# Two places for the transposed probabilities around the values' result, and another order of loads and of tiles 14 and 15, in a transformer layer

## The chip, the core and the metric

The kernel runs on one core of a Trainium2 chip. The metric is the device time of one execution in microseconds (us). Its engines are TensorE (PE; PEld is its weight load), VectorE (DVE), ScalarE (ACT), GpSimd (POOL) and SyncE (SP), whose queue issues the loads and stores (DMAs). Each engine takes its instructions in program order.

## What is computed

One layer over 2048 frames of 1024 channels, in float32. The input is scaled and shifted by vectors made from a conditioning vector c, and one projection makes u (512 channels) and q, k, v (8 heads of 64).

```python
h = x * (1.0 + sc1) + sh1
proj = h @ w_in                       # u, q, k, v
y_pool = pool_mixer(u, w_pool, pool_scale)                        # trailing means of 2/4/8/16 frames minus u
y_attn = chunked_attention(q, k, v, rel_bias)                     # 64-frame chunk: itself and 8 chunks before
y = concat([y_pool, y_attn]) @ w_out
x = layer_norm(ALPHA * x + (1.0 + g1) * y, ln1_g, ln1_b)
h = x * (1.0 + sc2) + sh2
f = jnp.square(relu(h @ w_ff1)) @ w_ff2
x = layer_norm(ALPHA * x + (1.0 + g2) * f, ln2_g, ln2_b)
```

## The kernel before

**Numbers.** Every float32 product is made of three matmuls: an operand is kept as a high part (a ScalarE copy to the matmul's rounded type) and a low part (source minus high part, on VectorE or GpSimd). `split` does both.

**Stages.** (1) `load0`, `chain0`, `fold0`, `dense0`: the modulation vectors and the first three blocks of the projection, `FIRST` = A0 (q and k of head 0), V0 (v of heads 0 and 1), U0, over the first 1024 frames. (2) Attention, together with the rest of the projection: a main loop over 128 units (two halves `hf` of 1024 frames, 8 heads, 8 query tiles of 128 frames). (3) `w_out`, residual and first layer norm for 16 tiles of 128 frames (`residual`, `ln1_head`, `ln1_turn`, `ln1_sums`). (4) The MLP in two phases of products over quarters (Strassen-like sums: 7 products for 8), 32 groups of the first one, `product(g, s)` with s from 0 to 6.

**The attention loop.** All order is written by hand: one iteration issues, for unit n, the scores of unit n + 3 (`scores`: S in PSUM, VectorE's reduction L611 into s and m, ScalarE's exponential L613), `normalise` on GpSimd, some matmuls of the projection taken from the generator `dense()` by `step`, then `transposes(n)` (up to five 128x128 blocks of s into T), in even iterations `values(n - 2)` (the product with v for the pair of units before, into pv, 256 columns), then `probs(n)` (high part of T on ScalarE, L635, low part on VectorE, L636, into PT), in even iterations `combine(n - 2)` (ScalarE copies rows 64 to 128 of pv to `yl`, L659; VectorE adds rows 0 to 64, L660), and more of `step`. `evac` brings a projection block out of its bank d in steps: for an A block ScalarE copies q (L300) and k (L301), VectorE makes the low parts (L303, L306).

**PSUM.** Eight banks of 512 float32 columns: left pool psL has d (three of one bank) and T (two banks, one buffer), right pool psR has S (two banks, one buffer) and pv (one bank). The MLP opens `psF0` in psR's place and, some products later, `psF1` in psL's place; `fbank()` deals their eight banks out in turn.

**Pieces.** While the projection's last blocks of the first half run, `h_pieces(tb)` replaces the modulated input in SBUF by that of the second half: a load into `xr` (four buffers), scale and shift (L271), high part (L273), low part (L275), 16 pieces in all, advanced at every second k of a projection block. `wo_pieces(n)` does the same for the scaled output weight `woS`, 8 pieces for each half n. `extras` makes further modulation vectors and `woS` in pieces that use `xr` as well.

**Tiles 14 and 15.** The layer norm of the last tiles overlaps the MLP's first group: `ln1_turn(t)` transposes tile t into T and writes the modulated h with eight ScalarE instructions (L832), `ln1_sums(t)` makes four VectorE sums and stores them, `op_split(i)` splits the operand of product i.

Of the kernel before, what the change touches and what calls it, by code (L numbers as in the profile page):

```python
# [8 lines left out]
F32 = mybir.dt.float32  # L9
# [15 lines left out]
def trunk_layer(ctx: ExitStack, tc: tile.TileContext, xT, x, wada1, wada2, vecs, rows, win, wfirst, wpT, wout,  # L25
# [111 lines left out]

    def dbank():
        return pp.tile([128, 512], F32, name="d", tag="d", bufs=3)

    def wide(tag):
        return (pr if tag == "S" else pp).tile([128, 1024], F32, name=tag, tag=tag, bufs=1)

    def narrow(w=512):
        return pr.tile([128, w], F32, name="pv", tag="pv", bufs=1)
# [7 lines left out]
             (2, 1): narrow()}  # L153
# [11 lines left out]
    def dense0(k):  # L165
        for i, (a, b) in enumerate(((0, 0), (1, 0), (0, 1))):
            for c in range(NF0):
                for tb in range(2):
                    nc.tensor.matmul(first[c, tb], wf[:, a, k, c, :], hT(b, k, slice(tb * 512, tb * 512 + 512)),  # L169
                                     start=(k == 0 and i == 0), stop=(k == 7 and i == 2))  # L170
# [81 lines left out]
    def xr_tile():  # L252
        while stores:
            stores.pop(0)()
        return ap.tile([128, 512], F32, name="xr", tag="xr", bufs=4)

    def h_pieces(tb):
        c0, cols = 1024 + tb * 512, slice(tb * 512, tb * 512 + 512)
        rs = {}

        def load(k):
            rs[k] = xr_tile()
            nc.sync.dma_start(rs[k], xT[k, :, c0:c0 + 512])

        for k in range(4):
            load(k)
        yield
        for k in range(10):
            if k < 8:
                r = rs[k]  # L270
                nc.gpsimd.tensor_scalar(r, r, mod1[:, k, 1:2], mod1[:, k, 0:1], op0=ALU.mult, op1=ALU.add)  # L271
            if 1 <= k < 9:
                nc.scalar.copy(hT(0, k - 1, cols), rs[k - 1])  # L273
            if k >= 2:
                nc.vector.tensor_sub(hT(1, k - 2, cols), rs.pop(k - 2), hT(0, k - 2, cols).bitcast(F32))  # L275
                if k + 2 < 8:
                    load(k + 2)
            if k < 7 or k == 9:
                yield
# [86 lines left out]
    for c, name in enumerate(FIRST):  # L366
        alloc(0, name[0], int(name[1]))
        g = both(c, name)
        pend.append((g, (0, name), name[0]))
# [30 lines left out]
    def dense():  # L400
        w, open_, side = {}, [], iter(())
        for hf, name, tb in blocks():
# [10 lines left out]
            prep = st.split_some(open_[0] + 2)  # L413
            if (hf, name, tb) in ((0, "U1", 1), (1, "A0", 0), (1, "A0", 1), (1, "U0", 1)):
                run(side)
                side = iter(()) if (hf, name, tb) == (1, "A0", 1) else wo_pieces(0) if (hf, name) == (1, "U0") else h_pieces(hf)
                next(side, None)
# [203 lines left out]
    def transposes(n):  # L621
        hf, h, i = units[n]
        s, m, nk = P.pop(n)
        e = i % 2
        t = wide("T")
        for j in range(nk):
            nc.tensor.transpose(t[:, j * 128:j * 128 + 128], s[:, j * 128:j * 128 + 128], ident)  # L627
        return t, e, nk
# [9 lines left out]
    def values(n):  # L638
        hf, h, i = units[n]
        gi = hf * 8 + i  # L640
        lo = 4 - min(gi, 4)
        pv = narrow(256)
        v = Vt[hf, h // 2]
        tot = 2 * (6 - lo)
        c = 0
        for sl in range(lo, 6):
            for a in range(2):
                nc.tensor.matmul(pv, v[:, i + sl, h % 2, :], PTt[:, a, sl, :], start=(c == 0), stop=(c == tot - 1))  # L648
                c += 1
        return pv  # L650
# [16 lines left out]
    def wo_pieces(n):  # L667
        run(ex[0])
        run(ex[1])
        flush()  # L670
        cols = slice(n * 512, n * 512 + 512)
        rs = {}

        def load(k):
            rs[k] = xr_tile()
            nc.sync.dma_start(rs[k], woS[k, :, cols])

        for k in range(4):
            load(k)
        yield  # L680
        for k in range(8):
            r = rs.pop(k)
            split(hT(0, k, cols), hT(1, k, cols), r, nc.vector if k % 2 else nc.gpsimd)
            if k + 4 < 8:
                load(k + 4)
            yield
# [137 lines left out]
    def ln1_turn(t, bank="T"):  # L824
# [6 lines left out]
        for k in range(8):  # L831
            nc.scalar.activation(h[:, k, :], pt[:, k * 128:k * 128 + 128], AF.Identity, bias=b2[:, k:k + 1],  # L832
                                 scale=a2[:, k:k + 1])
# [84 lines left out]
    q3 = [s3[:, 0:512], s3[:, 512:1024], narrow()]  # L918
# [89 lines left out]
    op_load(6)  # L1008
    op_split(4)
    ln1_sums(14, 1)  # L1010
# [12 lines left out]
    def fbank():  # L1023
        i = turn[0] % 8
        turn[0] += 1
        return pf[i >= 3].tile([128, 512], F32, name="f", tag="f", bufs=(3, 5)[i >= 3])
# [163 lines left out]
    for g in range(32):  # L1190
        for s in range(7):
            product(g, s)
            tick()
            if g == 0:
                if s == 1:
                    ln1_load(15)
                elif s == 2:
                    ln1_turn(15)
                elif s == 3:
                    ln1_sums(15, 1)  # L1200
                elif s == 4:
                    op_split(6)
                elif s == 5:
                    flush()
# [25 lines left out]
            evacuate(g, s)  # L1230
            if (g, s) == (0, 0):
# [214 lines left out]
```

## Time and profile before

| | |
|---|---|
| median of 3 runs | 2112.88 us (2112.39 to 2114.71) |
| the profiled execution | 2112.46 us, of which the span of instructions is 2110.6 |
| TensorE busy | 2037.9 us (97%) |
| VectorE, ScalarE, GpSimd busy | 1303.0, 1001.5, 333.3 us |

A busy TensorE is not one at its peak, since matmuls are pipelined and their ends are modelled. Idle time of an engine counts when the engine that sets the end waits for it. Start times in rows count from the start of the span.

### The profile page before, as it was taken

What the parts mean: (1) busy time and instruction counts of PE and PEld (TensorE: products, weight loads), DVE (VectorE), ACT (ScalarE), POOL (GpSimd) and SP (SyncE); (2) the same over time, 40 slices, a digit from 0 to 9 for tenths busy, and PEclk for the clock granted to TensorE, in tenths of its full rate; (3) what the DMA queues carried; (4) which work ended last, traced back from release to release, by engine and by line L of the source; (5) the groups of instructions that cost most, each with busy time, mean ns of one, the idle gap of its engine ahead of it and who ended that gap; (6) DMA issues with size and microseconds to landing.
All of it is one profiled execution on the core that took longest, in us unless ns stands there. A gap on an engine that the chain in (4) does not pass through costs nothing.

```text
span 2110.6 us, 27080 instructions
## 1 busy us (share of the span) xinstructions
PE 2037.9 (97%) x9672; PEld 1681.5 (80%) x9672; DVE 1303.0 (62%) x1958; ACT 1001.5 (47%) x1592; POOL 333.3 (16%) x442
## 2 busy tenths in 40 slices
PE   7999989999998999899999999999999999999998
PEld 6778868887877888678888788888788888888886
DVE  7555555556665464767776765666694447775448
ACT  5554555554553555545555655545453333333330
POOL 1535463553333100000000000000000001000002
PEclk9999999999999999999999999999999999999999
DMA  7444444434434678879878988887886556776552
GB/s 300 142 133 127 148 138 112 140 103 141 129 109 125 199 232 296 287 253 324 287 270 296 319 280 295 294 293 281 322 288 211 189 194 209 246 242 227 193 170 110
DMA packets 210360, 456.68 MB, mean 216 GB/s; under 512 B 18609, under 2 KB 36529, under 8 KB 209202
## 3 DMA queue, kind: packets, MB, share of 16 engines
q1 hardware_dynamic: 210226, 454.96, 64.2%
q8 instruction: 76, 1.25, 0.2%
q14 instruction: 58, 0.48, 0.1%
HBM read 294.45 MB, written 152.05 MB: 212 GB/s over the span
## 4 chain that ended last, share of the span: by engine, by line
PE 81%; DVE 7%; ACT 4%; DMA 3%; issue 3%; POOL 2%; SPq 0%; DVEq 0%; POOLq 0%; ACTq 0%
PE f L1331 26%; PE f L1049 26%; PE d L422 10%; PE d L386 6%; PE pv L648 3%; PE T L627 2%; PE S L604 2%; DVE s L611 1%; ACT PT L635 1%; PE d L169 1%; DMA raw<-in_wada_dram 1%; DVE PT L636 1%; DVE sb L60 1%; PE S L169 1%; PE S L386 1%
## 5 line engine op out<-in xcount | busy, mean ns | idle before, releaser
L1331 PE MATMUL f<-sb,sa 128*128 128x512 f32 x2688 | 616.3, 391 | 2.1 <-DVE sb L60 1.8
L1331 PEld LDWEIGHTS f<-sb,sa 128*128 128x128 f32 x2688 | 504.7, 188 | 113.6 <-DVE sb L60 2.5
L422 PE MATMUL d<-hT,hl 128*128 128x512 f32 x1392 | 373.5, 400 | 1.9 <-ACT vt L317 1.9
L1049 PE MATMUL f<-h,hl 128*128 128x512 f32 x1536 | 363.0, 391 | 2.0 <-ACT c L1056 1.2
L1049 PEld LDWEIGHTS f<-h,hl 128*128 128x128 f32 x1536 | 287.9, 188 | 67.9 <-ACT c L1056 2.1
L1049 PE MATMUL f<-sb,hl 128*128 128x512 f32 x1152 | 279.7, 396 | 11.6 <-ACT c L1056 8.1
L422 PEld LDWEIGHTS d<-hT,hl 128*128 128x128 f32 x1392 | 249.2, 190 | 42.2 <-ACT vt L317 2.3
L1049 PEld LDWEIGHTS f<-sb,hl 128*128 128x128 f32 x1152 | 218.0, 190 | 63.0 <-ACT c L1056 9.4
L636 DVE TENSOR_TENSOR PT<-T,PT 128x640 fp32r<-128x640 f32 (+4 forms) x128 | 94.9, 741 | 217.2 <-ACT PT L635 215.1
L613 ACT ACTIVATE s<-s,m 128x640 f32<-128x640 f32 (+4 forms) x128 | 97.9, 765 | 221.3 <-DVE m L611 171.2
L386 PE MATMUL d<-hT,hl 128*128 128x512 f32 x696 | 165.7, 394 | 0.0
L1071 ACT ACTIVATE g<-g 128x512 f32<-128x512 f32 x96 | 60.8, 633 | 210.5 <-DVE g L1062 210.5
L59 ACT CAST sb<-hl 128x1024 fp32r<-128x1024 f32 x67 | 70.4, 1051 | 177.7 <-PE f L1331 142.9
L386 PEld LDWEIGHTS d<-hT,hl 128*128 128x128 f32 x696 | 129.0, 188 | 26.9
L60 DVE TENSOR_TENSOR hl<-wsum,hl 128x1024 fp32r<-128x1024 f32 x64 | 78.4, 1225 | 92.9 <-ACT hl L59 92.9
L619 POOL TENSOR_SCALAR s<-s,m 128x640 f32<-128x640 f32 (+4 forms) x128 | 97.1, 759 | 240.0 <-DVE m L618 192.5
L60 DVE TENSOR_TENSOR sb<-hl,sb 128x1024 fp32r<-128x1024 f32 x67 | 81.9, 1222 | 69.0 <-ACT sb L59 68.8
L59 ACT CAST sb<-raw 128x1024 fp32r<-128x1024 f32 x53 | 55.5, 1052 | 119.2 <-PE f L1331 85.0
L1374 POOL TENSOR_SCALAR ag<-ag 128x1024 f32<-128x1024 f32 x1 | 1.1, 1060 | 666.9 <-DMA ab<-in_rows_dram 666.9
L604 PE MATMUL S<-k,q 128*128 128x320 f32 (+1 forms) x448 | 92.2, 322 | 12.8 <-DVE m L611 12.7
L1300 POOL TENSOR_SCALAR zv<-zv 128x1 f32<-128x1 f32 x16 | 16.7, 1042 | 554.7 <-DVE zv L1299 554.7
L60 DVE TENSOR_TENSOR hl<-w,hl 128x1024 fp32r<-128x1024 f32 x64 | 61.3, 958 | 68.3 <-ACT hl L59 68.3
(182 smaller groups left out, 2674.7 us busy)
## 6 DMA issues: line engine op xcount, KB each, us to landing
fS<-g SPq DMA_DIRECT2D x224, 256.0 KB, 3.9
hl<-fS SPq DMA_DIRECT2D x67, 512.0 KB, 4.7
hl<-tS SPq DMA_DIRECT2D x67, 512.0 KB, 4.7
w<-in_w_dram SPq DMA_DIRECT2D x48, 512.0 KB, 4.3
raw<-fS SPq DMA_DIRECT2D x45, 512.0 KB, 4.6
raw<-tS SPq DMA_DIRECT2D x45, 512.0 KB, 4.8
wS<-wsum SPq DMA_DIRECT2D x32, 512.0 KB, 4.8
raw<-in_w_dram SPq DMA_DIRECT2D x32, 512.0 KB, 5.2
```

The source lines that it names most:

```text
L59: nc.scalar.copy(hl_h, src)
L60: low.tensor_sub(hl_l, src, hl_h.bitcast(F32))
L386: nc.tensor.matmul(ps, yc[:, a, k, :], hT(b, k, cols), start=(k == 0 and i == 0), stop=(k == 7 and i == 2))
L422: nc.tensor.matmul(ps, w[name][:, a, k, :], hT(b, k, slice(tb * 512, tb * 512 + 512)), start=(n == 0), stop=(n == 23))
L604: nc.tensor.matmul(S[:, 512 * p:512 * p + wp], q[:, i * 128:i * 128 + 128], k[:, a, k0 + p * wp:k0 + p * wp + wp], start=(a == 0), stop=(a ...
L613: nc.scalar.activation(s[:, 0:w], s[:, 0:w], AF.Exp, bias=m[:, 0:1], scale=-1.0, accum_out=m[:, 1:2])
L619: nc.gpsimd.tensor_scalar(s[:, 0:nk * 128], s[:, 0:nk * 128], m[:, 1:2], 1.0, op0=ALU.mult, op1=ALU.mult)
L636: nc.vector.tensor_sub(ol, src, oh.bitcast(F32))
L648: nc.tensor.matmul(pv, v[:, i + sl, h % 2, :], PTt[:, a, sl, :], start=(c == 0), stop=(c == tot - 1))
L1049: nc.tensor.matmul(ps, w[:, p, c:c + 128], h[:, q, k, :], start=first and k == 0 and (p, q) == (0, 0), stop=k == 3 and p == 1, skip_group_ ...
L1071: nc.scalar.activation(o, o, AF.Relu)
L1331: nc.tensor.matmul(bank, f, w, start=start, stop=stop, skip_group_check=True)
```

## The change

In PSUM, left and right change places in part. The left pool holds one tile of three banks in a row, `tpv` (1536 columns). In attention the transposes of an even unit go to columns 0 to 640, those of an odd one to 896 to 1536, and the values' result to 640 to 896 between them; elsewhere columns 0 to 1024 serve as T and 1024 to 1536 as the single bank. The d banks move to the right pool; `fbank()` takes five banks from the right pool first and three from the left later.

V0's products end first in the last step of `dense0`, and its evacuation is first in line. `xr` has eight buffers. The pieces of x are loaded eight ahead, the first eight at the block before, and modulated on VectorE, not on GpSimd; those of the output weight are loaded eight ahead over both halves. A piece that is done loads the one six further on, into the buffer freed two pieces before. The sums of tile 14 stand before `op_split(4)`. The turn of tile 15 moves by one product, its eight ScalarE instructions follow that product's evacuation, and its sums and the closing of the pools move after `op_split(6)`.

```diff
+    tpv = pp.tile([128, 1536], F32, name="tpv")
     def dbank():
-        return pp.tile([128, 512], F32, name="d", tag="d", bufs=3)
+        return pr.tile([128, 512], F32, name="d", tag="d", bufs=3)
     def wide(tag):
-        return (pr if tag == "S" else pp).tile([128, 1024], F32, name=tag, tag=tag, bufs=1)
-    def narrow(w=512):
-        return pr.tile([128, w], F32, name="pv", tag="pv", bufs=1)
+        return pr.tile([128, 1024], F32, name="S", tag="S", bufs=1) if tag == "S" else tpv[:, 0:1024]
...
     def dense0(k):
+        order = [(i, c, tb) for i in range(3) for c in range(NF0) for tb in range(2)]
+        if k == 7:
+            order = [(i, c, tb) for c in (1, 0, 2) for tb in range(2) for i in range(3)]
...
-        return ap.tile([128, 512], F32, name="xr", tag="xr", bufs=4)
+        return ap.tile([128, 512], F32, name="xr", tag="xr", bufs=8)
+    def pieces(source):
+        rs = {}
+        def load(j):
+            if j < 16:
+                rs[j] = xr_tile()
+                nc.sync.dma_start(rs[j], source(j))
+        def pop(j):
+            rs.pop(j)
+            if j >= 2:
+                load(j + 6)
+        return rs, load, pop
+    hp_rs, hp_load, hp_pop = pieces(lambda j: xT[j % 8, :, 1024 + j // 8 * 512:1536 + j // 8 * 512])
+    wp_rs, wp_load, wp_pop = pieces(lambda j: woS[j % 8, :, j // 8 * 512:j // 8 * 512 + 512])
     def h_pieces(tb):
-        for k in range(4):
-            load(k)
         yield
         for k in range(10):
             if k < 8:
-                nc.gpsimd.tensor_scalar(r, r, mod1[:, k, 1:2], mod1[:, k, 0:1], op0=ALU.mult, op1=ALU.add)
+                nc.vector.tensor_scalar(r, r, mod1[:, k, 1:2], mod1[:, k, 0:1], op0=ALU.mult, op1=ALU.add)
...
-    for c, name in enumerate(FIRST):
+    for c, name in sorted(enumerate(FIRST), key=lambda v: (1, 0, 2)[v[0]]):
...
+            if (hf, name, tb) == (0, "A7", 0):
+                for j in range(8):
+                    hp_load(j)
...
-        t = wide("T")
+        t = tpv[:, 896 * e:896 * e + 640]
...
-        pv = narrow(256)
+        pv = tpv[:, 640:896]
...
     def wo_pieces(n):
+        if n == 0:
             run(ex[0]); run(ex[1]); flush()
+            for j in range(8):
+                wp_load(j)
...
+    ln1_sums(14, 1)
     op_split(4)
-    ln1_sums(14, 1)
...
-        return pf[i >= 3].tile([128, 512], F32, name="f", tag="f", bufs=(3, 5)[i >= 3])
+        return pf[i >= 5].tile([128, 512], F32, name="f", tag="f", bufs=(5, 3)[i >= 5])
...
             if g == 0:
-                elif s == 2:
-                    ln1_turn(15)
                 elif s == 3:
-                    ln1_sums(15, 1)
+                    turned = ln1_turn(15, later=True)
                 elif s == 4:
                     op_split(6)
                 elif s == 5:
+                    ln1_sums(15, 1)
+                elif s == 6:
                     flush()
                     psL.__exit__(None, None, None)
...
             evacuate(g, s)
+            if (g, s) == (0, 3):
+                turned()
```

## Rows read from the trace of the kernel before

**Rows 1.** The page, its head

```profile
span 2110.6 us, 27080 instructions
```

**Rows 2.** TensorE's waits, whole span: us in total, times, longest us

```profile
PE T L627 <- DVE PT L636: 13.5, 16, 2.5
PE S L604 <- DVE m L611: 12.7, 12, 2.2
...
PE f L1049 <- ACT c L1056: 9.3, 3, 5.8
...
PE d L422 <- ACT vt L317: 1.9, 1, 1.9
```

**Rows 3.** Windows: us, busy PE, PEld, DVE, ACT, POOL, clock, DMA share, GB/s

```profile
282.00:331.00 49.00, 39.02 (x195) 32.14 (x194) 27.40 (x60) 27.48 (x57) 30.41 (x36) 0.93 0.59 164
619.00:663.00 44.00, 38.77 (x226) 32.88 (x225) 25.97 (x50) 24.84 (x48) 24.20 (x27) 0.99 0.41 126
```

**Rows 4.** TensorE's waits from 284 to 345

```profile
PE S L604 <- DVE m L611: 3.5, 2, 2.2
PE T L627 <- DVE PT L636: 3.5, 2, 2.5
PE T L627 <- POOL hl L60: 3.3, 2, 3.0
```

**Rows 5.** Line 271 (min/median/max ns); what it waited for, who waited for it

```profile
L271 POOL TENSOR_SCALAR xr<-xr,mod x16: 763/774/1435, 282.9 to 329.2; 128x512 f32<-128x512 f32 x16
...
  DMA xr<-in_xT_dram: 9.2, 4
...
  ACT hT L273: 13.9, 10
```

**Rows 6.** Line 488, the same operation and shape on VectorE

```profile
L488 DVE TENSOR_SCALAR xa<-xr,cs x6: 469/478/506, 83.3 to 544.9; 128x512 f32<-128x512 f32 x6
```

**Rows 7.** Line 303: what VectorE sat idle for before it

```profile
  ACT k L301: 21.6, 30
```

**Rows 8.** Order of time at 402: start, us, engine, line, operation

```profile
401.92 0.37 ACT L659 COPY yl<-pv 64x256 f32<-64x256 f32 x1
401.93 0.82 DVE L636 TENSOR_TENSOR PT<-T,PT 128x640 fp32r<-128x640 f32 x1 [1.70 <-ACT PT L635]
402.67 0.41 DVE L660 TENSOR_TENSOR y<-pv,yl 64x256 f32<-64x256 f32 x1
...
403.09 0.71 PE L627 MATMUL T<-ident,s 128*128 128x128 f32 x5
```

**Rows 9.** Order of time at 392, two units earlier

```profile
392.04 0.82 DVE L636 TENSOR_TENSOR PT<-T,PT 128x640 fp32r<-128x640 f32 x1 [2.52 <-ACT PT L635]
...
394.53 0.71 PE L627 MATMUL T<-ident,s 128*128 128x128 f32 x5
```

**Rows 10.** TensorE's waits from 635 to 672

```profile
PE T L627 <- DVE PT L636: 5.2, 4, 2.3
```

**Rows 11.** Tile xr, 600 to 670: one wait of ScalarE for it

```profile
  DMA xr<-woS: 4.8, 3
```

**Rows 12.** Order of time at the MLP's entrance

```profile
843.39 5.88 PE L1049 MATMUL f<-h,hl 128*128 128x512 f32 x25
...
845.42 1.28 DVE L873 SCALAR_TENSOR_TENSOR xt<-xt,d 128x512 f32<-128x512 f32 x2
...
854.62 0.68 DVE L1062 TENSOR_TENSOR g<-f,c 128x512 f32<-128x512 f32 x1
...
857.14 2.90 ACT L832 ACTIVATE h<-T,b,a 128x128 f32<-128x128 f32 x8 [3.69 <-DMA hP<-h]
...
859.89 0.66 ACT L1071 ACTIVATE g<-g 128x512 f32<-128x512 f32 x1
...
862.26 4.47 PE L1049 MATMUL f<-sb,hl 128*128 128x512 f32 x12 [5.84 <-ACT c L1056]
...
870.47 3.00 PE L1049 MATMUL f<-sb,hl 128*128 128x512 f32 x12 [0.98 <-DVE g L1062]
```

More of the change, by code (lines that the diff above doesn't have):

```diff
@@ L152, in trunk_layer @@
     first = {(0, 0): s0[:, 0:512], (0, 1): s0[:, 512:1024], (1, 0): dbank(), (1, 1): dbank(), (2, 0): dbank(),
-             (2, 1): narrow()}
+             (2, 1): tpv[:, 1024:1536]}
     ld = {}
@@ L165, in dense0 @@
     def dense0(k):
[L166 to L170, printed above, removed]
+        order = [(i, c, tb) for i in range(3) for c in range(NF0) for tb in range(2)]
+        if k == 7:
+            order = [(i, c, tb) for c in (1, 0, 2) for tb in range(2) for i in range(3)]
+        for i, c, tb in order:
+            a, b = ((0, 0), (1, 0), (0, 1))[i]
+            nc.tensor.matmul(first[c, tb], wf[:, a, k, c, :], hT(b, k, slice(tb * 512, tb * 512 + 512)),
+                             start=(k == 0 and i == 0), stop=(k == 7 and i == 2))
     acs = {}
@@ L254, in xr_tile @@
             stores.pop(0)()
-        return ap.tile([128, 512], F32, name="xr", tag="xr", bufs=4)
-    def h_pieces(tb):
[L258 to L263, printed above, removed]
-        for k in range(4):
-            load(k)
+        return ap.tile([128, 512], F32, name="xr", tag="xr", bufs=8)
[12 more added lines that the diff above has]
+    wp_rs, wp_load, wp_pop = pieces(lambda j: woS[j % 8, :, j // 8 * 512:j // 8 * 512 + 512])
+    def h_pieces(tb):
+        cols = slice(tb * 512, tb * 512 + 512)
         yield
@@ L269, in h_pieces @@
             if k < 8:
-                r = rs[k]
-                nc.gpsimd.tensor_scalar(r, r, mod1[:, k, 1:2], mod1[:, k, 0:1], op0=ALU.mult, op1=ALU.add)
+                r = hp_rs[8 * tb + k]
+                nc.vector.tensor_scalar(r, r, mod1[:, k, 1:2], mod1[:, k, 0:1], op0=ALU.mult, op1=ALU.add)
             if 1 <= k < 9:
-                nc.scalar.copy(hT(0, k - 1, cols), rs[k - 1])
+                nc.scalar.copy(hT(0, k - 1, cols), hp_rs[8 * tb + k - 1])
             if k >= 2:
-                nc.vector.tensor_sub(hT(1, k - 2, cols), rs.pop(k - 2), hT(0, k - 2, cols).bitcast(F32))
-                if k + 2 < 8:
-                    load(k + 2)
+                j = 8 * tb + k - 2
+                r = hp_rs[j]
+                nc.vector.tensor_sub(hT(1, k - 2, cols), r, hT(0, k - 2, cols).bitcast(F32))
+                hp_pop(j)
             if k < 7 or k == 9:
@@ L667, in wo_pieces @@
     def wo_pieces(n):
-        run(ex[0])
-        run(ex[1])
-        flush()
         cols = slice(n * 512, n * 512 + 512)
[L672 to L679, printed above, removed]
+        if n == 0:
+            run(ex[0])
+            run(ex[1])
+            flush()
+            for j in range(8):
+                wp_load(j)
         yield
         for k in range(8):
[L682 to L685, printed above, removed]
+            split(hT(0, k, cols), hT(1, k, cols), wp_rs[8 * n + k], nc.vector if k % 2 else nc.gpsimd)
+            wp_pop(8 * n + k)
             yield
@@ L822, in ln1_load, with ln1_turn @@
             nc.sync.dma_start(hps[t], hP[b][0][r - 4])
-    def ln1_turn(t, bank="T"):
+    def ln1_turn(t, bank="T", later=False):
         n = n_tiles.pop(t)
@@ L830, in ln1_turn, with affine @@
         hts[t] = h = h_tile(t, "h")
-        for k in range(8):
-            nc.scalar.activation(h[:, k, :], pt[:, k * 128:k * 128 + 128], AF.Identity, bias=b2[:, k:k + 1],
-                                 scale=a2[:, k:k + 1])
+        def affine():
+            for k in range(8):
+                nc.scalar.activation(h[:, k, :], pt[:, k * 128:k * 128 + 128], AF.Identity, bias=b2[:, k:k + 1],
+                                     scale=a2[:, k:k + 1])
+        if later:
+            return affine
+        affine()
     def ln1_sums(t, delay=12):
@@ L917, in trunk_layer @@
     s3 = wide("S")
-    q3 = [s3[:, 0:512], s3[:, 512:1024], narrow()]
+    q3 = [s3[:, 0:512], s3[:, 512:1024], tpv[:, 1024:1536]]
     for t in range(3):
```

## The prediction, made before the changed kernel was run

> **What bounds the kernel now.** I read the page's head first, then TensorE's waits over the whole span, then the same waits cut to the stretches in which the diff puts an edit, and last the order of time around single waits. The span is 2110.6 us [rows 1]; the profiled execution took 2112.46 us, 0.42 under the median of 2112.88, and every sum below is made against 2112.46. TensorE is the engine that sets the end, so a microsecond saved elsewhere counts only where TensorE stands still for it. The waits in reach are: 13.5 us of the probabilities' transposes (T) for VectorE's low part of the unit before (PT, L636), 12.7 us of the scores for VectorE's reduction, 9.3 us of MLP products for a ScalarE copy, 1.9 us of a projection for the copy `vt` [rows 2]. The MLP phases, from 843.39 on [rows 12] six tenths of the span, are touched at their entrance alone. A measurement of this kernel tells about 0.2% (4.2 us) from no change.
>
> **Start.** The kernel's first projection to need a bank waits 1.9 us for `vt` [rows 2], which ScalarE makes third, behind A0's two copies. V0 now comes first: two of three about equal copies leave the front, 2/3 x 1.9 = 1.3 saved. At most 1.9, at least 0 (the other copies may then be waited for). The reordered k = 7 products are the same 18 matmuls: nothing.
>
> **The x pieces (282 to 331).** TensorE's waits from 284 to 345 sum to 3.5 + 3.5 + 3.3 = 10.3 us [rows 4], and the granted clock's mean over 282 to 331 is 0.93 [rows 3], where 7% of 49 us is another 3.4 us of work at full speed. What stands behind them: the modulation (L271) runs on GpSimd, 16 times at 774 ns or more, waits 9.2 us for loads, and ScalarE waits 13.9 us for it [rows 5]; ScalarE's queue also holds the next PT copy, VectorE waits for that, and T for VectorE. The change removes the 16 GpSimd instructions, loads eight pieces one block ahead, and reloads two slots behind the one just freed, so that SyncE's queue need not stand on a buffer just being released. It adds 16 VectorE tensor_scalars of the same 128x512 shape, 478 ns by L488 [rows 6]: 7.6 us. Nothing hides these fully: VectorE goes from 27.4 to 35.0 us busy in that stretch, and TensorE needs 39.0 - 3.4 = 35.6 [rows 3]. On SyncE's queue eight loads move ahead of one block's copies and stores; their buffers are free, so they hold it for eight issues only, and the copies of k, wanted a block later, are covered by that block's matmuls (uncovered, they would add a wait for scores). The least it can shrink to is 35.6 of 49, which agrees with 10.3 + 3.4 = 13.7 as the most that is saved. Two engines of equal load that wait for each other in queues don't close up entirely; the other end is VectorE's own 7.6 in TensorE's path, with only the 3.3 that [rows 4] put down to GpSimd itself bought back: +4 (a loss). I take 5 saved: ScalarE's wait of 13.9 goes, VectorE's 7.6 comes, and the difference, 6.3, is shortened for the reductions (L611) that now queue behind a modulation on VectorE and that the scores wait for.
>
> **The output weight's pieces (619 to 663).** Four T waits, 5.2 us together, lie from 635 to 672 [rows 10]; ScalarE waits 4.8 us in 3 cases for the scaled weight's load [rows 11], with the PT copy behind it in its queue. Work on the engines stays as it was; loads go out eight deep and the second half's during the first. VectorE has room (25.97 of 44 [rows 3]). Gain between 0 and 5.2; I take 3.5, since the fourth wait comes after the loads are in.
>
> **Tiles 14 and 15 at the MLP's entrance.** Today the fifth product of the first group waits 5.84 us and starts at 862.26. The copy of c that it waits for stands on ScalarE behind eight affine instructions (2.90 us from 857.14), which themselves waited for the store of tile 14, and behind the square pair that starts at 859.89 [rows 12]. After the change the affine stands behind the copy of the fourth product. The square then follows VectorE's sum of 854.62 + 0.68 = 855.30; from square to product it takes 862.26 - 859.89 = 2.37 today, so the fifth product starts at 857.67. What is late next is the seventh: today 862.26 + 8.21 = 870.47 [rows 12]. The four VectorE sums of tile 15 (0.68 each, like the sum at 854.62), 2.7 in all, leave its path for a place behind the evacuation; the affine and one copy (2.90 + 0.6) enter ScalarE's queue ahead of the split that the seventh needs. 857.67 + 8.21 - 2.7 + 3.5 = 866.7: 3.8 saved. The sums of tile 14 before op_split(4) send the stores of tile 14 some 2.5 us earlier, which covers the slot that the affine writes. The other bound is in the banks: the first five MLP banks now take the place of S and of the three d banks, which the residual of tile 15 reads until 845.42 + 1.28 = 846.70, while the first product starts at 843.39 [rows 12]. If the first product gets one of these, 3.3 of the 3.8 are lost again. S was allocated before d, so I take it that it doesn't.
>
> **The two fields.** T(even) takes columns 0 to 640, the values' result 640 to 896, T(odd) 896 to 1536: the middle bank of 512 holds the last transpose of even units, the values' result, and the first transpose of odd ones. What the trace shows of neighbours in a bank: VectorE's q (L303) reads rows 0 to 64 of d and needs ScalarE's first copy alone, yet 30 times it waits for the second copy (L301), which reads the other rows: 21.6 us [rows 7]. So I take accesses of two engines to one bank to be kept in program order, reads included. Then an even unit that waits for PT(n-1) gets its first four transposes out early, 4/5 of 0.71 = 0.57 at most, while the fifth and the values wait as before. An odd unit gets worse: `yl` may read only when L636 is done (today both start at 401.92) and L660 follows; T(odd), which today needs L636 alone, needs both. That is 0.37 + 0.41 = 0.78 later [rows 8]. Where TensorE leads it costs nothing: 392.04 + 0.82 to 394.53 are 1.67 to spare [rows 9]. Where the spare is 0.34 (402.75 to 403.09 [rows 8]) it costs 0.44. Behind the waiting `yl` stand the next evacuation copies and the exponential on ScalarE. Of 16 waits [rows 2] 2 + 4 are counted in the two stretches above; 10 x 0.57 = 5.7 relief, against some ten tight pairs at 0.44 to 0.78, about 6.5. Net +1; bounds -7 (no cost, also 16 x 0.44 of relief) and +12.5 (16 x 0.78, no relief).
>
> The Trainium skill has the rule in its page "PSUM — Partial Sum Buffer", section "PSUM bank collisions raise a hardware error": two engines may not touch the same bank in the same 32 partitions at once, reads against reads and other columns included, so waits are to be set by bank. This speaks against a layout with a shared middle bank. By this rule the term is the +1 above, and by columns alone it would be about -6; the trace's row agrees with it, and is even stricter, as its two readers use different partitions.
>
> **Sum.** -1.3 - 5 - 3.5 - 3.8 + 1 = -12.6; 2112.46 - 12.6 = 2099.9, said as 2100. The extra attention slots (xr 8 for 4) in the weight extras are costed at nothing: their loads are issued two jobs ahead and lie under projections; if that cover is gone the cost is at most a stall as now.
>
> **The rivals.**
> - Both stretches close up to TensorE's pace: 13.7 and 5.2 in place of 5 and 3.5: 2112.46 - 1.3 - 13.7 - 5.2 - 3.8 + 1 = 2089.5. For it: the waits shown have GpSimd and loads behind them, and both go. Against it: VectorE at 35.0 beside TensorE's 35.6.
> - The fields part by columns: term -6 for +1, 2093. Against it: [rows 7].
> - VectorE becomes the bound of the x stretch (+4 there): 2112.46 - 1.3 + 4 - 3.5 - 3.8 + 1 = 2108.9, within 0.2%. For it: 7.6 us more in its queue, in front of L611.
> - The change doesn't do what it says, that is, the loads and GpSimd were hidden by the same VectorE chain, and both stretches stay: 2112.46 - 1.3 - 3.8 + 1 = 2108.4, at the edge of no change. Against it: the 9.2 and 4.8 us of waits for loads.
> - Slower: the combination enters the loop of every pair. At 0.78 for 40 of 64 pairs (128 units) it costs 31, in place of 1: 2130. It decides from 18 over the gains' 13.6 + 4.2, which is 23 tight pairs. For it: the order in [rows 7]. Against it: only 16 T waits in 128 units, and 1.67 of room in the steady ones.
>
> **Chances.** Forecast 0.46, closing up 0.2, columns 0.1, VectorE bound 0.1, stretches stay 0.08, slower 0.06. The forecast's own range is 2092 to 2107. The two cases near 2108.5 lie on the line between faster and same, so a third of them counts as faster: faster 0.82, same 0.12, slower 0.06. The range: the closing case together with the columns ends near 2082, and of these I leave the lower part out; above, VectorE bound is in. 2085 to 2110.
>
> **What would show it.** Start: the wait for `vt` under 0.8 us. Stretches: no L271 on GpSimd, no wait for xr loads, TensorE's waits between 280 and 330 about 5 us and a clock of 1.0; if the S waits for L611 grow there, VectorE is the bound. Entrance: fifth product without a wait of over 3 us, seventh about 4 us nearer to the first. Fields: `yl` starting after L636's end, T waits before odd units on L660, few before even ones; waits on L636 in both would refute the order by bank. The prediction is wrong if the pair's period in the steady stretch (380 to 400) grows, or if the first MLP product waits for tile 15's residual.

## The result, and the profile after

The changed kernel takes 2150.82 us (median of 5 runs, 2146.24 to 2152.62) against 2112.88: a ratio of 1.0167 [1.0152, 1.0182], by which it is 35 us slower (the two medians are 37.9 apart), where 2100 was forecast. The head of the page after:

```profile
span 2149.0 us, 26977 instructions
```

TensorE's waits over the whole span (us in total, times, longest). In the new numbering T's transposes are L646, the low part of PT is L655, the reduction L630, `yl` L678 and the addition to y L679:

```profile
PE S L623 <- DVE m L630: 23.5, 21, 3.0
PE tpv L646 <- DVE y L679: 13.8, 15, 2.4
...
PE tpv L646 <- DVE PT L655: 9.6, 13, 2.0
PE f L1067 <- ACT c L1074: 5.2, 3, 2.4
PE f L1067 <- DVE g L1080: 4.2, 3, 2.6
PE f L1067 <- DVE xt L891: 3.3, 1, 3.3
```

Against [rows 2]: the scores wait 23.5 us where they waited 12.7, the transposes 13.8 + 9.6 = 23.4 where they waited 13.5 for the low part alone, and 15 of these waits are for the addition, which they never waited for before. In the order of time all 15 stand before odd units and all 13 for the low part before even ones. The MLP's wait for the copy of c is down from 9.3 to 5.2, and a new one of 3.3 stands at its door. The attention's loop is where the time goes: set against the trace of before, the first transpose of unit 0 comes 0.4 us later, of unit 32 6.9, of unit 64 12.4, of unit 96 21.8, of unit 127 33.9. From the first transpose of one unit to that of the next there are 127 steps: 43 of them are longer by over 0.3 us, by 41.1 in sum, 6 are shorter by over 0.3, by 8.9, and 70 agree within 0.1. Taken by pairs, from one even unit's first transpose to the next one's, 35 of 63 periods are longer by over 0.3 us, by 35.3 in sum.

What one such step looks like, in order of time (start, us, engine, line, operation):

```profile
416.02 0.82 DVE L655 TENSOR_TENSOR PT<-tpv,PT 128x640 fp32r<-128x640 f32 x1 [1.69 <-ACT PT L654]
416.88 0.37 ACT L678 COPY yl<-tpv 64x256 f32<-64x256 f32 x1 [0.89 <-DVE PT L655]
417.28 0.42 DVE L679 TENSOR_TENSOR y<-tpv,yl 64x256 f32<-64x256 f32 x1 [0.44 <-ACT yl L678]
417.62 0.81 DVE L630 CUSTOM_DVE_ANT_0 s<-S,bias 128x640 f32<-128x640 f32 x1
...
417.84 0.74 PE L646 MATMUL tpv<-ident,s 128*128 128x128 f32 x5 [0.95 <-DVE y L679]
```

In [rows 8] `yl` and the low part start together, the addition follows at once, and T comes 0.34 us after the low part's end. Here `yl` waits for the low part's end, VectorE stands idle while `yl` runs, the addition ends at 417.70 and T comes after that. ScalarE's and VectorE's waits from 60 to 700 show that this is so in nearly every one of the 64 pairs. ScalarE first, then VectorE:

```profile
ACT yl L678 <- DVE PT L655: 51.3, 63, 1.3
```

```profile
DVE y L679 <- ACT yl L678: 27.0, 62, 0.4
```

In the x pieces' stretch (here 292 to 341) and the output weight's (here 650 to 697), in the columns of [rows 3]:

```profile
292.00:341.00 49.00, 38.92 (x193) 30.74 (x192) 36.16 (x77) 26.66 (x57) 20.42 (x20) 0.93 0.51 142
...
650.00:697.00 47.00, 41.74 (x234) 35.35 (x233) 28.06 (x51) 25.85 (x50) 24.72 (x27) 0.96 0.31 96
```

VectorE is busy for 36.2 us of 49 (27.4 in [rows 3]), and the clock is still 0.93. The modulation is L286 now (what waited for it below the first line):

```profile
L286 DVE TENSOR_SCALAR xr<-xr,mod x16: 519/528/1125, 292.3 to 337.7; 128x512 f32<-128x512 f32 x16
...
  ACT hT L288: 1.3, 1
```

So 528 ns each on VectorE (478 were counted), and ScalarE's wait for the modulated piece fell from the 13.9 us of [rows 5] to 1.3. The MLP's entrance, to be read beside [rows 12] (38.5 us later at its first product):

```profile
880.43 1.28 DVE L891 SCALAR_TENSOR_TENSOR xt<-xt,d 128x512 f32<-128x512 f32 x2
...
881.86 10.02 PE L1067 MATMUL f<-h,hl 128*128 128x512 f32 x36 [3.28 <-DVE xt L891]
...
891.08 0.63 ACT L1089 ACTIVATE g<-g 128x512 f32<-128x512 f32 x1 [1.89 <-DVE g L1080]
...
895.27 3.01 PE L1067 MATMUL f<-sb,hl 128*128 128x512 f32 x12
895.56 2.91 ACT L846 ACTIVATE h<-tpv,b,a 128x128 f32<-128x128 f32 x8 [0.29 <-PE tpv L841]
...
903.67 2.53 PE L1067 MATMUL f<-sb,hl 128*128 128x512 f32 x10 [2.63 <-DVE g L1080]
```

The affine stands behind the copies, the fifth product starts at 895.27 without a wait, the seventh at 903.67. From first to seventh that is 21.8 us, where [rows 12] have 870.47 - 843.39 = 27.1; the 3.3 in front of the first product take part of that back. (The last row is cut short by the end of the view: the product has 12 matmuls.)

### The profile page after: what moved, and what is told of

Read it like the earlier page. It is cut to its first block, busy times and chain, and to the rows that moved or that the text cites. A ratio compares the mean times of both kernels' runs of the same rounds, so it can differ in the third digit from the quotient of the medians.

```text
span 2149.0 us, 26977 instructions
## 1 busy us (share of the span) xinstructions
PE 2053.5 (96%) x9672; PEld 1685.3 (78%) x9672; DVE 1316.8 (61%) x1974; ACT 1000.6 (47%) x1592; POOL 322.1 (15%) x426
## 4 chain that ended last, share of the span: by engine, by line
PE 73%; DVE 11%; ACT 6%; issue 4%; DMA 3%; POOL 1%; SPq 0%; DVEq 0%; POOLq 0%; ACTq 0%
PE f L1351 26%; PE f L1067 26%; PE d L402 6%; PE d L441 6%; PE tpv L667 2%; DVE s L630 2%; ACT PT L654 2%; DVE PT L655 2%; PE tpv L646 2%; PE S L623 1%; DVE xa L509 1%; ACT s L632 1%; DVE k L322 1%; PE d L172 1%; ACT yl L678 1%
## 5 line engine op out<-in xcount | busy, mean ns | idle before, releaser
L655 DVE TENSOR_TENSOR PT<-tpv,PT 128x640 fp32r<-128x640 f32 (+4 forms) x128 | 94.9, 741 | 216.3 <-ACT PT L654 216.2
L623 PE MATMUL S<-k,q 128*128 128x320 f32 (+1 forms) x448 | 93.7, 325 | 23.6 <-DVE m L630 23.5
L646 PE MATMUL tpv<-ident,s 128*128 128x128 f32 x560 | 85.8, 280 | 27.3 <-DVE y L679 13.8
L646 PEld LDWEIGHTS tpv<-ident,s 128*128 128x128 f32 x560 | 66.6, 144 | 57.0 <-issue 27.2
L623 PEld LDWEIGHTS S<-k,q 128*128 128x128 f32 x448 | 74.2, 189 | 47.0 <-DVE m L630 35.0
```

The costliest lines, as they stand in the source:

```text
L623: nc.tensor.matmul(S[:, 512 * p:512 * p + wp], q[:, i * 128:i * 128 + 128], k[:, a, k0 + p * wp:k0 + p * wp + wp], start=(a == 0), stop=(a ...
L655: nc.vector.tensor_sub(ol, src, oh.bitcast(F32))
```

## The experiments

The kernel before ran beside every group of runs, with a median near 2113 us, and differences are worked out as ratio less 1, times 2113.

**Which part is it?** Two kernels split the change: one adds these lines to the kernel before, the other takes them out of the changed kernel. (Where lines are left out of an edit, `...` stands for them.)

```diff
+    tpv = pp.tile([128, 1536], F32, name="tpv")
...
-        return pp.tile([128, 512], F32, name="d", tag="d", bufs=3)
+        return pr.tile([128, 512], F32, name="d", tag="d", bufs=3)
...
-        t = wide("T")
+        t = tpv[:, 896 * e:896 * e + 640]
...
-        pv = narrow(256)
+        pv = tpv[:, 640:896]
...
-        return pf[i >= 3].tile([128, 512], F32, name="f", tag="f", bufs=(3, 5)[i >= 3])
+        return pf[i >= 5].tile([128, 512], F32, name="f", tag="f", bufs=(5, 3)[i >= 5])
```

> The kernel before with the two fields, the values' result between them and the d banks on the other side, and none of the other edits. Theory M (the values' result shares its place with the probabilities: the copy yl waits for the low part L636, L660 for yl, and the next odd transposes for L660): the attention stage loses what it lost in the changed kernel, some 34 us, and the first MLP product waits 3 us for tile 15's residual: 2145 to 2156 us. Rival P (the x pieces' modulation on VectorE and the deeper loads lengthen VectorE's queue, and the fields cost nothing): 2109 to 2117 us.

2151.87 us, 1.0177 [1.0161, 1.0194]. From the first transpose of unit 0 to that of unit 127 it takes 38 us longer than before. TensorE's waits are those of after:

```profile
PE S L605 <- DVE m L612: 20.7, 20, 2.0
PE tpv L628 <- DVE y L661: 16.3, 17, 2.6
PE tpv L628 <- DVE PT L637: 12.3, 14, 2.0
```

> The changed kernel with the PSUM layout of before (one T of two banks, pv in its own bank, d on the left), all other edits kept. Theory M: the 34 us are gone and the other edits show what they are worth, 8 to 14 us: 2098 to 2105 us; no wait of yl for the low part. Rival P: 2140 us or more.

2108.55, 0.9975 [0.9965, 0.9986]. The whole loss lies in the fields, and what is left of the change gains 5 us, not 13.6, and less than the 8 to 14 that I expected of this run.

**Is it the field, the sharing, or where the banks lie?** Three kernels, none with two fields.

```diff
+    tp = pp.tile([128, 1024], F32, name="tp")
...
-        return (pr if tag == "S" else pp).tile([128, 1024], F32, name=tag, tag=tag, bufs=1)
+        return pr.tile([128, 1024], F32, name="S", tag="S", bufs=1) if tag == "S" else tp
...
-        pv = narrow(256)
+        pv = tp[:, 640:896]
```

> The kernel before with one field only, T, as a tile that stays, and the values' result in the unused columns 640 to 896 of its second bank; d, S and everything else as before. Theory M: sharing alone costs, without any second field: yl waits for L636 about 0.8 us in each of 64 pairs, and the kernel takes 2140 to 2156 us. Rival S (the cost is in the second field, whose transposes write while the other field is read): no cost, 2110 to 2117 us.

2149.31, 1.0170 [1.0155, 1.0185]: one field and the values' result in T's second bank costs as much as the two fields.

```diff
+    tp = pp.tile([128, 1024], F32, name="tp")
...
-        return (pr if tag == "S" else pp).tile([128, 1024], F32, name=tag, tag=tag, bufs=1)
+        return pr.tile([128, 1024], F32, name="S", tag="S", bufs=1) if tag == "S" else tp
```

> The kernel before, with T as one tile that stays in place of a new one for each unit, and the values' result in its own bank as before. Theory M (the loss is the order of the values' readers against the probabilities' readers): no change, 2110 to 2117 us, and no wait of yl for L636. Rival S (a tile that stays orders its users more strictly than a new one, whoever they are): 2125 us or more.

2114.52, 1.0000 [0.9991, 1.0009]: a T that stays allocated costs nothing while the values keep a bank, and a tile, of their own.

```diff
-        return pp.tile([128, 512], F32, name="d", tag="d", bufs=3)
+        return pr.tile([128, 512], F32, name="d", tag="d", bufs=3)
...
-        return pr.tile([128, w], F32, name="pv", tag="pv", bufs=1)
+        return pp.tile([128, w], F32, name="pv", tag="pv", bufs=1)
...
-        return pf[i >= 3].tile([128, 512], F32, name="f", tag="f", bufs=(3, 5)[i >= 3])
+        return pf[i >= 5].tile([128, 512], F32, name="f", tag="f", bufs=(5, 3)[i >= 5])
```

> The kernel before with d in the right pool beside S, T and pv in the left one, and the MLP's banks dealt five and three; no fields. Theory M: attention as before, and the first MLP product waits some 3.3 us for the residual of tile 15, part of which later waits give back: 2113 to 2117 us. Rival P expects the same as before, 2112 to 2114 us, and no such wait.

2113.38, 1.0000 [0.9990, 1.0010]. The first MLP product comes 3.45 us later, as after, and the fifth then waits 2.46 us in place of 5.84; at the twentieth product 0.4 is left. So neither the second field nor the banks' places cost anything, but the sharing does. In these kernels the values' result shares T's bank and T's tile at once; which of the two makes the engines wait they don't tell apart.

**Does the order of the readers matter?** Four readers stand between two products of the shared banks: the copy and the low part of PT read T, `yl` and the addition read the values.

```diff
+        if pv is not None:
+            combine(n - 2, pv)
         if t:
             probs(*t)
-        if pv is not None:
-            combine(n - 2, pv)
```

> The kernel fields_alone, with the two readers of the values' result (yl, L660) written ahead of the two readers of the probabilities (L635, L636) of the same iteration; places and sizes as they were. Theory M (within the shared place users keep the order in which they are written, so yl stood behind L636 and the odd transposes behind L660): yl runs while VectorE waits for L635 anyway, the odd transposes wait for L636 alone as before, and L635 is later by some 0.3 us where it follows L660: 2113 to 2130 us. Rival B (readers of one bank on two engines cost time in any order): 2140 us or more.

2144.07, 1.0138 [1.0121, 1.0155]. My theory then was that only T's wait for the addition cost; it asked for 2113 to 2130 and missed. ScalarE's waits from 60 to 700 show what took its place: the PT copy now waits for the addition.

```profile
ACT PT L636 <- DVE y L661: 34.2, 63, 3.0
```

The same edit in the kernel before:

> The kernel before with only this order (yl and L660 ahead of L635 and L636); the values' result in its own bank. Theory M: nothing waits for another reader here; VectorE's 0.41 us of L660 move into the time in which it waits for L635, ScalarE's 0.37 of yl stand ahead of L635: 2107 to 2116 us. Rival B: the same as before, since no bank is shared: 2110 to 2116 us. This one is the control for fields_combine_first.

2119.30, 1.0026 [1.0016, 1.0035]: the order alone, with banks of their own, costs 5.5 us, more than I expected, and 29.2 - 5.5 = 24 remain for the sharing in this order. So the theory became: four readers in one chain, whichever comes first. It was put to a third order, with the values' readers one unit later.

```diff
+        if held and n % 2:
+            combine(*held.pop())
         if t:
             probs(*t)
         if pv is not None:
-            combine(n - 2, pv)
+            held.append((n - 2, pv))
+        if held and n >= NU:
+            combine(*held.pop())
```

> Two fields alone, with the two instructions that read a pair's values' result (ACT yl, DVE addition) held back by one unit: they stand behind the odd unit's transposes and ahead of its PT copy. If what costs is that the four readers of the three banks (PT copy, PT low part, yl, addition) are put one behind another wherever they stand between two products, this moves the chain from the odd unit's transposes to the even unit's and the time stays at 2140 to 2156. If it costs only because the odd unit's transposes wait for the addition, that wait is gone, and the time is 2113 to 2130.

2142.50, 1.0147 [1.0133, 1.0161], as the chain asks. T no longer waits for the addition at all, and yet most of the loss stays: 31 us (this order without a shared bank was not tried). ScalarE's wait, from 60 to 700, is again that of the copy for the addition, and T's waits for the low part, 13.5 us in [rows 2], are 40.2 over the whole span:

```profile
ACT PT L636 <- DVE y L661: 32.5, 63, 2.4
```

```profile
PE tpv L628 <- DVE PT L637: 40.2, 36, 5.8
```

**Take readers out of the chain.**

```diff
-        yl = ap.tile([64, 256], F32, name="yl", bufs=1)
+            nc.gpsimd.memset(ysb[hf, h], 0.0)
...
-        nc.scalar.copy(yl, pv[64:128])
-        nc.vector.tensor_add(y[:, i * 128:i * 128 + 256], pv[0:64], yl)
```

> Before with the two readers of the values' result left out (no yl, no addition; y is zero, so half of the attention's output is left out). Yardstick for the next one. Its readers lie beside the PT low part and ahead of the slack, so on either theory it changes little: 2095 to 2114 us.

2104.29, 0.9955 [0.9942, 0.9968]: the two readers by themselves take 9.5 us of the kernel before.

> Two fields alone, with the same two readers left out. If the cost is the chain of four readers between two products of the shared banks, the cost is gone with two of the four: within 0 to 10 us of the kernel before without readers. If the cost is that the values' product lies in the bank that T's copies read, and the readers don't matter, 20 to 37 us above that kernel remain.

2106.03, 0.9964 [0.9951, 0.9977]. The 37 us shrink to 0.0009 x 2113 = 1.9, which the intervals don't tell from nothing: the values' product in the shared bank costs little or nothing by itself. Its readers do.

```diff
-        nc.scalar.copy(yl, pv[64:128])
-        nc.vector.tensor_add(y[:, i * 128:i * 128 + 256], pv[0:64], yl)
+        nc.vector.tensor_copy(y[:, i * 128:i * 128 + 256], pv[0:64])
```

> Two fields alone, with one reader of the values' result in place of two: VectorE copies the upper half (about 0.4 us), ScalarE's yl and the sum of halves are left out. By the chain of readers the step behind the PT low part shrinks from 0.37 + 0.42 and two hand-overs (some 0.9 to 1.2 us) to some 0.45: a cost of 8 to 20 us in place of 37, so 2115 to 2135 us. If the readers don't matter, 2140 or more.

2114.75, 1.0003 [0.9994, 1.0012]: as fast as the kernel before, which has `yl` and the addition, and just below what I expected. What sharing costs here can only be bounded, since the kernel before with one reader was not run: leaving out both readers gave 9.5 us, so leaving out `yl` can have given anything up to that, and sharing with one reader costs between 0.6 and 10 us. It isn't free: T waits for the copy in 8 cases, over the whole span:

```profile
PE tpv L628 <- DVE y L659: 5.7, 8, 1.9
```

In order of time, the step that stands beside the one at 416 after:

```profile
404.24 0.82 DVE L637 TENSOR_TENSOR PT<-tpv,PT 128x640 fp32r<-128x640 f32 x1 [1.70 <-ACT PT L636]
404.98 0.41 DVE L659 COPY y<-tpv 64x256 f32<-64x256 f32 x1
405.31 0.81 DVE L612 CUSTOM_DVE_ANT_0 s<-S,bias 128x640 f32<-128x640 f32 x1
405.54 0.74 PE L628 MATMUL tpv<-ident,s 128*128 128x128 f32 x5
```

T follows the copy by 0.15 us here too, but its start is 1.30 after the low part's start, against 1.82 after and 1.16 in [rows 8], and VectorE has no hole: the reduction starts 1.07 after the low part's start, as in the trace of before at that place, against 1.60 after. So most of the cost comes with `yl`, which has two sides: half a microsecond of VectorE's and TensorE's way, and a place in ScalarE's queue with other copies behind it.

```diff
-        nc.scalar.copy(yl, pv[64:128])
+        nc.vector.tensor_copy(yl, pv[64:128])
```

> Two fields alone, with yl copied by VectorE in place of ScalarE: the way from the PT low part to the odd unit's transposes keeps its length (0.4 + 0.4 us on VectorE in place of 0.37 + 0.42 with short hand-overs), but nothing waits in ScalarE's queue. If the length of that way sets the cost, the time stays at 2135 to 2155 us; if the cost is ScalarE's queue standing behind yl, 2110 to 2122 us.

2138.32, 1.0121 [1.0107, 1.0134]: the length of the way sets most of it (25.6 of 37.4 us); the 11.8 that went can be put down to ScalarE's queue. The way did keep its length: from the low part's end to the addition's end it takes 0.91 us here and 0.85 with the fields alone (medians of 64; 0.32 before). TensorE's waits from 60 to 840:

```profile
PE tpv L628 <- DVE PT L637: 13.2, 15, 2.0
PE tpv L628 <- DVE y L661: 12.1, 12, 2.5
PE S L605 <- DVE m L612: 10.9, 14, 2.0
```

The waits for the addition stay; those of the scores are half of the 20.7 of the fields alone.

**What is the rest worth?** Each remaining part by itself, as it stands in the diff.

```diff
+            order = [(i, c, tb) for c in (1, 0, 2) for tb in range(2) for i in range(3)]
...
+    for c, name in sorted(enumerate(FIRST), key=lambda v: (1, 0, 2)[v[0]]):
```

> Before with the start edit alone (the last eighth of the first three dense products goes chunk by chunk, and their evacuation begins with chunk 1). By the step-by-step comparison of the run that has all but the fields, the edit itself was worth +0.4 to +1.2 us at unit 0: 2112 to 2115 us. By the prediction's term of -1.3 us: 2111 to 2112.

2113.50, 1.0002 [0.9993, 1.0011]: nothing. The projection's wait of 1.9 us for `vt` became one of 1.1 by the V transposes and one of 0.7 by the projection.

```diff
+        return ap.tile([128, 512], F32, name="xr", tag="xr", bufs=8)
...
+                nc.vector.tensor_scalar(r, r, mod1[:, k, 1:2], mod1[:, k, 0:1], op0=ALU.mult, op1=ALU.add)
...
+                wp_load(j)
```

> Before with the x and the output weight's pieces as after (eight slots, loads a block ahead, modulation on VectorE), and nothing else. By the steps read in the run without the fields (-2.3 in the x stretch, -2.2 in the other), 2107 to 2110 us. If the entrance gave the gain there, 2112 to 2114.

2110.49, 0.9988 [0.9979, 0.9996]: a gain of 2.5 us, just short of the 3 to 6 expected.

```diff
+                elif s == 3:
+                    turned = ln1_turn(15, later=True)
...
+            if (g, s) == (0, 3):
+                turned()
```

> Before with only the other order of tiles 14 and 15 at the entrance of the MLP. By the prediction's term (-3.8 us) and the -3.7 us read between the first products in the run without the fields, 2108 to 2110.5 us. If that gain was only a shift of the pieces' gains or of a half-clock stretch, 2112 to 2114.

2112.58, 0.9998 [0.9989, 1.0007]: missed. In its trace the way from the first to the seventh product is indeed 3.7 us shorter (+3.48 us against before at the first, -0.20 at the seventh), and 28 products after the first it is 1.9 behind again. The granted clock (third column from the end) of two short stretches in between:

```profile
870.70:874.10 3.40, 3.40 (x10) 2.62 (x9) 3.37 (x7) 0.72 (x2) 0.00 (x0) 0.50 0.40 157
908.30:911.70 3.40, 3.40 (x8) 2.72 (x9) 3.37 (x5) 1.38 (x2) 0.00 (x0) 0.50 1.00 365
```

Both stretches are at 1.2 GHz, each right behind a wait of TensorE (2.68 and 2.28 us). The trace of before has such stretches too, at 858.5 and 906.3. The other part of what is given back is new waits: the fourteenth product waits 0.7 us for VectorE's addition here, and 1.5 and 1.7 us in the two other runs that have this edit with the banks as before (all but the fields, and the next one below), where the tenth product also waits 0.6 us for ScalarE's copy. The kernel before and the runs with the start edit alone and the pieces alone, which keep the old order, have neither wait. From the first to the thirtieth product those two runs are 2.6 and 2.1 us shorter than the profiled execution of before without this edit; the three runs with it are 1.6, 3.4 and 3.6 us shorter. So little of the 3.7 is left by then.

> All of the change but the fields and but the start edit. If the start edit gives nothing or costs about a microsecond, 2105 to 2109 us, at or a little below the run with all but the fields (2108.6); if it was worth the 1.3 us of the prediction, 2109 to 2111.

2108.22, 0.9977 [0.9968, 0.9986]: some 5 us faster than before, like all but the fields; the interval overlaps that of the pieces alone as well.

```diff
-                nc.vector.tensor_scalar(r, r, mod1[:, k, 1:2], mod1[:, k, 0:1], op0=ALU.mult, op1=ALU.add)
+                nc.gpsimd.tensor_scalar(r, r, mod1[:, k, 1:2], mod1[:, k, 0:1], op0=ALU.mult, op1=ALU.add)
```

> The kernel all_but_fields with the modulation of the x pieces put back on GpSimd; eight slots and early loads stay. Theory L (the loads and SyncE's queue were what the x stretch waited for, and VectorE's 7.6 us of modulation cost most of what they gained): the same or faster than all_but_fields by up to 3 us, 2105 to 2109 us. Rival G (GpSimd's queue, with 1.3 us splits ahead of the modulations, was what ScalarE waited for): slower than all_but_fields by 2 to 5 us, 2110 to 2114 us.

2108.75, 0.9968 [0.9957, 0.9979], beside 0.9975 [0.9965, 0.9986] for the same kernel with the modulation on VectorE: the engine of the modulation makes no difference that could be told apart, so what the stretch gains comes with the slots and the loads. TensorE's waits from 282 to 345 are 9.2 us in this trace, 3.8 of them for GpSimd's split `hl`.

> The x and output weight's pieces and the entrance as after, the banks as before, and yl on VectorE. Each pair takes 0.4 us from ScalarE and gives it to VectorE, which is the busier of the two in the attention's loop: 2106 to 2114 us, more likely no better than the version with yl on ScalarE (2108.2).

2119.60, 1.0030 [1.0018, 1.0042], above what I expected: without any shared bank, 0.4 us more on VectorE (and 0.37 less on ScalarE) in each of 64 pairs costs (1.0030 - 0.9977) x 2113 = 11.2 us. It shows how little room VectorE has in these pairs.

## Why the prediction was wrong

| step | predicted, us | measured, us |
|---|---|---|
| start | -1.3 | +0.4 [-1.5, +2.3] |
| x pieces and output weight's pieces | -5 - 3.5 = -8.5 | -2.5 [-4.4, -0.8] |
| tiles 14 and 15 | -3.8 | -0.4 [-2.3, +1.5] in the time, -3.7 at the place |
| two fields | +1 | +37.4 [+34.0, +41.0] |
| all | -12.6 | +35.3 [+32.1, +38.5] |

**The two fields** are the step that failed: the sum had them at +1, and they measured +37.4. The reading behind the term was right where it decided the sign: reads are kept in order too, `yl` follows the low part, and T before odd units waits for the addition. Wrong were the price of a pair, with it the number of pairs that pay, and the relief.

*The price.* "Where TensorE leads it costs nothing" counts T's lateness alone, and that is the smaller part. I had measured T's spare time at two places, 1.67 and 0.34 us [rows 8, 9]. Over the whole trace of before, 16 of 63 odd units have less than 0.78 us between the end of the low part and their first transpose, and the term's own formula gives 8.0 us for them, not far from the 6.5 that I took. In the changed kernel none starts less than 1.0 us behind; to bring them all there takes 11.8 us, a third of the 37.4. The rest was put at nothing without a reason. VectorE stands idle for `yl` (27.0 us in 62 waits), so that the reduction and with it the next scores and exponential are late too, and `yl` holds ScalarE's queue, with the copies behind it that the prediction names but doesn't price. A pair can pay for that without any wait of T for the addition: 35 of 63 pair periods are longer, by 35.3 us, where the term had some ten at 0.44 to 0.78. Of the 29 steps in which VectorE also makes the low part of k for a projection block, 21 are longer, by 19.7 us; of the 29 in which VectorE has the unit's own work alone, 3 are, by 1.6. The steady stretch that I named as the sign, units 67 to 71, loses 0.0. The rival "the combination enters the loop of every pair", with 40 pairs and +31, came near in both numbers and had a chance of 0.06.

As an estimate from runs whose bases differ: 11 us for VectorE alone being 0.4 later (the last run), 25.6 - 11.2 = 14 more where T is later as well (fields with `yl` on VectorE), 12 for ScalarE's queue. No run takes these parts singly. Some of each comes through the clock, which the term left out. From the first transpose of unit 0 to that of unit 127, before and then after, in the columns of [rows 3]:

```profile
72.20:665.90 593.70, 564.07 (x3186) 478.25 (x3185) 334.37 (x743) 309.95 (x630) 267.51 (x329) 0.99 0.44 128
72.60:699.80 627.20, 577.46 (x3186) 481.22 (x3184) 347.43 (x759) 308.94 (x630) 256.29 (x313) 0.98 0.41 121
```

The same 3186 matmuls keep TensorE busy 13.4 us longer and leave it idle 20.1 longer. Stretches at 1.2 GHz, each behind a wait of TensorE, add up to 27.3 us after and 10.2 before; 17.1 us at half the clock are, as an estimate from these, up to 8.5 us.

*The relief* of 5.7 didn't come, and I had said "few before even ones": 13 of the 28 waits of T for the low part or the addition stand before even units. They stand ahead of the first of the five transposes and not of the fifth (at 385.48 us for 0.90), though the first goes to a bank that the unit before doesn't use. The traces show a reason: these waits are for a semaphore that the other engine's instruction raises, and the program sets them for a whole tile, not for a bank. In `dense0` of the changed kernel the sixth matmul of a step writes columns 1024 to 1536 of `tpv`, and in 7 of 8 steps its weight load waits on VectorE's semaphore, though all that VectorE reads of `tpv` in that stage is columns 0 to 2, two banks away (L194). In the trace of before the same matmul writes `pv`, a tile of its own, and never has that wait. In [rows 7] d is one bank and one tile, so they couldn't tell the two rules apart. A layout in which the fields and the values' result are separate tiles wasn't tried.

The Trainium skill's page "PSUM — Partial Sum Buffer", section "PSUM bank collisions raise a hardware error", has waits set by bank and 32 partitions, reads against reads included, and so spoke against the layout. The trace agrees as far as `yl` goes: it reads rows 64 to 128 and waits for the low part, which reads all 128, 51.3 us in 63 waits. The waits before even units go further than that rule, and the page has no price.

**The pieces** were over-sized, and the rival that the stretches mostly stay was nearer. ScalarE's wait went as said (13.9 to 1.3), but in the run without the fields TensorE's waits from 282 to 345 are

```profile
PE S L622 <- DVE m L629: 6.5, 3, 2.9
PE T L645 <- DVE PT L654: 1.7, 2, 1.3
```

8.2 us where [rows 4] have 10.3, now mostly for VectorE's reduction, and the clock there is still 0.93. GpSimd's place was taken by VectorE's queue: a wait was moved more than removed. Read from the first transposes of units 50 and 60, the x pieces gain 2.3 us in that trace where 5 were forecast; from those of units 116 and 127, the output weight's pieces gain 2.2 where 3.5 were.

**The entrance** was right up to the seventh product, 3.7 for 3.8, yet the sum stopped there: the tenth and fourteenth products then wait 0.6 and 1.5 us for the work that was moved behind, and too small a part reaches the end. I had taken it that S's banks go to the first product; in the changed kernel it waits 3.28 us for the residual of tile 15, the bound that I named and set aside. That costs nothing that the time shows (1.0000 [0.9990, 1.0010] with swapped banks), and in that trace the fifth product waits 3.4 us less.

**Start**: 2/3 x 1.9 was to be saved; the wait for `vt` only changed its place, 1.1 + 0.7 us for 1.9.

Alone, the parts sum to 0.4 - 2.5 - 0.4 + 37.4 = 34.9, close to the 35.3 measured; the 5.3 that all but the fields gain together would leave 32, and the intervals don't tell these apart.

## What to carry to other kernels

Before two results share a tile in PSUM, list all readers of the tile on all engines between two products and add them as one chain, with what each engine would have done meanwhile; in both orders tried here, moving two of them forward or back moved the chain and kept most of its cost. Count the pairs in which the chain is longer than the spare time of any engine in it, step by step over the trace, and not the waits that TensorE already has. A wait that was taken from GpSimd's queue and given to VectorE's, by then nearly as busy as TensorE (36.2 and 38.9 us of 49), paid a small part of what the wait was worth. Where a wait is shortened, follow the products behind it until the trace agrees with the old one again.

## What the runs showed that I had not expected

- The order is kept for the whole tile: two fields in one tile are no second buffer, though most of their columns lie in different banks.
- With one reader of the values' result in place of two, the kernel with the fields is as fast as before (1.0003 [0.9994, 1.0012]); how much of that is `yl` being gone is open.
- The readers' order alone, with banks apart, cost 5.5 us (1.0026 [1.0016, 1.0035]).
- TensorE's clock fell to 1.2 GHz for short stretches right behind waits of 1 to 3 us, also deep in the MLP: in the run of the start edit at 1191.1 us, behind gaps of 1.08 and 0.76 us, where the execution before has gaps of 1.58 and 0.76 and no such stretch. Such stretches come and go between profiled executions and move one by some microseconds, as much as the gains of three of the four steps here.
